# HGRN2 layer of a two-layer backbone: sum-free products first in the seven-product blocks, heads in a written order, four states in one PSUM bank

## The chip, the cores and the metric

The kernel runs on one core of one Trainium2 chip. The metric is the device time of one execution in microseconds (us). Before the change it is 3423.19 us, the median of 3 runs (3419.49 to 3425.61).

A core has five engines that run their own queues side by side. TensorE (PE) multiplies, VectorE (DVE) and GpSimd (POOL) work element by element, ScalarE (ACT) casts and evaluates functions, and SyncE (SP) issues most DMAs. An instruction waits at the head of its queue for semaphores of others, and what stands behind it in that queue waits too.

## The reference

Two layers over 1024 latent and 256 context tokens of width 1024. Layer 0 (neighbourhood attention beside an mLSTM) is not touched. Layer 1 is a bidirectional HGRN2 with 16 heads, key and value width 128 each:

```python
def _c_mixer(h_lat, h_ctx, w_in, lb, h_norm, w_out, need_ctx):
    def project(h):
        q, f_fwd, f_bwd, i, z = _split_cols(h @ w_in, C_SIZES)

        def decay(f_pre):
            f = lb + (1.0 - lb) * jax.nn.sigmoid(f_pre.astype(F32))
            return _bht(_heads(1.0 - f, HG_HEADS)), _bht(_heads(jnp.log(f), HG_HEADS))
        ...
    rec_l, z_l = project(h_lat)
    rec_c, z_c = project(h_ctx)
    o_l, o_c = _gla_bidir(rec_l, rec_c, need_ctx)
    ...

    def step(S, xs):
        qc, kc, vc, lfc = xs
        b = jnp.cumsum(lfc, axis=2)
        o = jnp.einsum('bhtk,bhkv->bhtv', qc * jnp.exp(b), S)
        pair = jnp.exp(jnp.where(tri, b[:, :, :, None, :] - b[:, :, None, :, :], -jnp.inf))
        a = jnp.einsum('bhtk,bhtsk->bhts', qc, pair * kc[:, :, None, :, :])
        o = o + jnp.einsum('bhts,bhsv->bhtv', a, vc)
        bL = b[:, :, -1:, :]
        S = jnp.exp(bL[:, :, 0])[..., None] * S + jnp.einsum('bhsk,bhsv->bhkv', kc * jnp.exp(bL - b), vc)
        return S, o
```

The gates f (forward and backward), q, values i and output gates z are projections of the normed tokens. In each direction a state S of 128 by 128 is carried from chunk to chunk; the context tokens give its start.

## The kernel before

**Products.** A dense fp32 product is three products of a high and a low part: hi by hi, hi by lo, lo by hi (`dense`, L131 to L133). `split` makes the parts: ScalarE casts (L73), VectorE subtracts (L74). So every weight block costs a cast and a subtraction before TensorE can use its low part.

**The passage into layer 1.** The normed tokens `hh`, `hl` (L317, L318) are made while layer 0's output projection ends. The backward gates of head 0 (`hg_f`, tiles mm, L983) are projected. Then `hg_wide` computes q and the forward gates of all heads in 16 blocks of two heads, each by seven products of half size instead of eight (one Strassen-like level). For this `half_sums` forms four sums S1 to S4 of quarters of the tokens (44 operations on VectorE, 12 on GpSimd, with the splits st1 to st4), and each block forms sums t1 to t4 of its weight quarters on GpSimd (L1072). The raw weights (`br`, DMAs at L1065) and the half sums share one ring of ten buffers. A unit of q comes first, and its products stand in the order (0,0), t2, (1,0), t3, t1, t4, (1,1). Products on S2 follow the first one. Their tails (L1048) add partial results; the forward-gate blocks also compute context parts of 256 columns (tiles tr). Results go to DRAM (`qd`, `fd`).

**A head.** `hg_intra` forms K = 1 - F (L1226), gkn (L1233), Q = q F (L1235), and then the causal matrix of each 128-token chunk in a binary scheme: the diagonal and seven levels. Each is a run of 16 strip matmuls (L1256); after it VectorE updates Q and K (L1303), F's running product (L1307), and merges the strips into gD (L1309). `hg_vz` projects context values, then values and output gates in eight token tiles of 24 products; `hg_close` transposes K (L1268); `hg_ctx` computes the states that the context gives (L1215); `hg_scan` carries the states. In the scan a u = K'V (L1323 backward, L1339 forward) goes into a PSUM bank of its own, three banks in turn, and VectorE makes the next state gS from it (L1325, L1341). The output acc sums three matmuls a chunk (L1334 to L1336), four chunks in the one acc bank, and VectorE multiplies it with the gate into gA (L1354). Transposes (L1393) follow. `hg_proj` loads the next head's q and f and projects its backward gates.

**Order.** Instructions are put on the engines by a scheduler that works on the written program with priorities: what is marked `urgent` (the strips) goes first, projections fill what is left. A pool's buffers are waited for as a whole unless it says otherwise.

## Time and profile before

| | before |
|---|---|
| median of 3 runs | 3423.19 us |
| the profiled execution: its time | 3423.08 us |
| its span | 3421.3 us |
| mean granted TensorE clock | 0.995 |
| DMA | 379.82 MB, mean 111 GB/s |

The span runs from the first to the last instruction in the trace. A row of a timeline gives start, time and the group of instructions, with the idle time ahead of it and what ended that in brackets. A row of the waits gives the waiting engine and line, who ended the wait, the sum, the number of times and the longest. A row of groups gives line, engine, operation, tiles, shapes and count, then busy time and the mean of one in ns. A row of the windows gives for each engine the busy time and the number of instructions in a stretch. Matmul records are pipelined, so their starts, not their lengths, give the pace.

### The profile page before, as it was taken

To read this page: it belongs to the slowest core of one execution; us is meant where nothing else is said; L and a number is where in the kernel's file an instruction comes from. 1 tells how busy PE (TensorE), PEld (TensorE's weight loads), DVE (VectorE), ACT (ScalarE), POOL (GpSimd) and SP (SyncE) were. 2 spreads that over 40 slices of the span, in tenths; PEclk is the share of its full clock that TensorE was granted. 3 is DMA by queue.
4 is the path that set the end of the run, shared out by engine and by line. 5 is a ranking of instruction groups with operands and counts; after the bars stand their busy time and mean duration, and the time that the engine had idled before them with its cause. 6 is when DMAs were issued, how large, how long until landed. Compare 5 with 4: busy or idle time off the path is not lost. (4 is left out here: it accounts for less than half of the span.)

```text
span 3421.3 us, 64930 instructions
## 1 busy us (share of the span) xinstructions
PE 3324.6 (97%) x24814; PEld 2927.6 (86%) x24814; DVE 2186.1 (64%) x4965; ACT 1454.6 (43%) x3389; POOL 834.7 (24%) x1215
## 2 busy tenths in 40 slices
PE   7999999999999999999997999999999999999999
PEld 6699899988899888898885888888888889889887
DVE  5346666666645576686667555665676576667757
ACT  5335554445534444454453333333333333333343
POOL 2222222222221121221015333112332242233110
PEclk9999999999999999999998999999999999999999
DMA  7612322223234443444742322322222233333357
GB/s 246 233 50 82 86 83 72 82 71 91 82 93 128 127 136 107 124 142 140 244 123 74 105 101 98 106 67 83 88 94 91 81 98 84 85 86 92 83 173 207
DMA packets 338103, 379.82 MB, mean 111 GB/s; under 512 B 34600, under 2 KB 269800, under 8 KB 336768
## 3 DMA queue, kind: packets, MB, share of 16 engines
q1 hardware_dynamic: 286032, 236.73, 23.6%
q0 software_dynamic: 51760, 138.94, 12.8%
q8 instruction: 195, 3.19, 0.4%
q14 instruction: 116, 0.95, 0.1%
HBM read 272.31 MB, written 103.08 MB: 110 GB/s over the span
## 5 line engine op out<-in xcount | busy, mean ns | idle before, releaser
L131 PE MATMUL mm<-wh,hh 128*128 128x256 f32 (+1 forms) x1504 | 464.2, 309 | 1.9 <-DVE graw L1535 0.7
L132 PE MATMUL mm<-wl,hh 128*128 128x256 f32 (+1 forms) x1504 | 462.9, 308 | 0.0
L133 PE MATMUL mm<-wh,hl 128*128 128x256 f32 (+1 forms) x1504 | 459.9, 306 | 0.0
L131 PE MATMUL mm<-hh,wh 128*128 128x512 f32 (+1 forms) x1096 | 400.3, 365 | 12.8 <-ACT wh L73 12.2
L133 PE MATMUL mm<-hh,wl 128*128 128x512 f32 (+1 forms) x1096 | 396.1, 362 | 3.1 <-DVE wl L74 3.1
L132 PE MATMUL mm<-hl,wh 128*128 128x512 f32 (+1 forms) x1096 | 396.9, 362 | 1.6 <-DVE hl L318 1.6
L131 PEld LDWEIGHTS mm<-wh,hh 128*128 128x128 f32 x1504 | 283.6, 189 | 21.1 <-ACT ev L352 3.4
L132 PEld LDWEIGHTS mm<-wl,hh 128*128 128x128 f32 x1504 | 283.6, 189 | 12.6 <-issue 0.7
L133 PEld LDWEIGHTS mm<-wh,hl 128*128 128x128 f32 x1504 | 283.5, 188 | 12.0 <-issue 0.5
L131 PE MATMUL mm<-wzh,hh 128*128 128x256 f32 x960 | 275.0, 287 | 0.7 <-DVE gz L1189 0.4
L132 PE MATMUL mm<-wzl,hh 128*128 128x256 f32 x960 | 275.2, 287 | 0.0
L133 PE MATMUL mm<-wzh,hl 128*128 128x256 f32 x960 | 274.8, 286 | 0.0
L131 PEld LDWEIGHTS mm<-hh,wh 128*128 128x128 f32 x1096 | 207.5, 189 | 47.9 <-ACT wh L73 12.6
L133 PEld LDWEIGHTS mm<-hh,wl 128*128 128x128 f32 x1096 | 207.2, 189 | 33.8 <-DVE wl L74 3.8
L132 PEld LDWEIGHTS mm<-hl,wh 128*128 128x128 f32 x1096 | 207.5, 189 | 31.9 <-DVE hl L318 4.3
L1286 ACT COPY gksel<-gK 128x1024 f32<-128x1024 f32 x96 | 110.8, 1154 | 193.8 <-PE s L1256 112.9
L131 PEld LDWEIGHTS mm<-wzh,hh 128*128 128x128 f32 x960 | 183.4, 191 | 2.7 <-DVE gz L1189 0.9
L132 PEld LDWEIGHTS mm<-wzl,hh 128*128 128x128 f32 x960 | 183.6, 191 | 1.6
L133 PEld LDWEIGHTS mm<-wzh,hl 128*128 128x128 f32 x960 | 183.4, 191 | 0.9
L1303 DVE TENSOR_TENSOR gQ<-gQ,gF 128x1024 f32<-128x1024 f32 x112 | 142.0, 1268 | 46.5 <-PE s L1256 46.1
L74 DVE TENSOR_TENSOR wl<-wraw,wh 128x512 fp32r<-128x512 f32 x176 | 120.0, 689 | 77.9 <-ACT wh L73 75.4
L1303 DVE TENSOR_TENSOR gK<-gK,gF 128x1024 f32<-128x1024 f32 x112 | 143.0, 1276 | 5.3 <-DVE gF L1307 0.5
(557 smaller groups left out, 8607.9 us busy)
## 6 DMA issues: line engine op xcount, KB each, us to landing
wraw<-in_wab_dram SPq DMA_DIRECT2D x108, 256.0 KB
wraw<-yd SPq DMA_DIRECT2D x92, 256.0 KB
br<-in_wc_dram SPq DMA_DIRECT2D x64, 256.0 KB
md<-ev POOLq DMA_DIRECT2D x60, 256.0 KB, 2.7
wraw<-in_wc_dram SPq DMA_DIRECT2D x120, 128.0 KB
mloz<-md SPq DMA_DIRECT2D x40, 256.0 KB
s<-gyt POOLq DMA_DIRECT2D x36, 256.0 KB, 5.0
adar<-in_wada_dram SPq DMA_DIRECT2D x16, 512.0 KB
```

The source lines that it names most:

```text
L74: nc.vector.tensor_tensor(out=lo, in0=x, in1=hi.bitcast(F32), op=ALU.subtract)
L131: mm(ps, lhsT=lh(k), rhs=rh(k), start=(start and k == 0), stop=False, skip_group_check=skip)
L132: mm(ps, lhsT=lh(k), rhs=rl(k), start=False, stop=False, skip_group_check=skip)
L133: m = mm(ps, lhsT=ll(k), rhs=rh(k), start=False, stop=(stop and k == nk - 1), skip_group_check=skip)
L1286: m = nc.scalar.copy(ksel.rearrange("p (b s i) -> p b s i", s=2, i=h), pick(K))
L1303: nc.vector.tensor_tensor(out=v, in0=v, in1=tot, op=ALU.mult)
```

## The change

**Half sums.** `half_sums` keeps its sums in the first half of F and in two working tiles instead of the ring, so the ring (now eleven) holds weights only; GpSimd's sum goes into output buffers. The counts of operations stay. It is called after the first three weight blocks have been asked for.

**Seven-product blocks.** A unit of gates comes first. Its products stand as (0,0), (1,0), t4, t2, t3, t1, then (0,1) and (1,1); t4 has an accumulator of its own. So three products and their context parts need no half sum. Tails are added in place. The pools wait tile by tile.

**Heads.** Context values (`hg_vt`) come ahead of the strips; each of the eight value tiles is issued after a strip run; the next head's gates are issued after the last run; the context states are placed after level 2; K's update stands ahead of a level's strips. In the scan four u's share one PSUM bank.

```diff
-    def half_sums(self, pool, tp):
+    def half_sums(self, pool, tp, F):
...
+        x = [F[:, 0, 0:512], F[:, 0, 512:1024]] + [self.t(tp, [P, 512], F32, n, 1) for n in ("u2", "u3")]
...
-        self.brs = 10
-        S = self.half_sums(sp, tp)
+        self.brs = 11
...
-        units = [(kind, i) for i in range(8) for kind in "qf"]
-        order = lambda kind: [(0, 0), "t2", (1, 0), "t3", "t1", "t4"] + ([(0, 1)] if kind == "f" else []) + [(1, 1)]
+        units = [(kind, i) for i in range(8) for kind in "fq"]
+        order = lambda kind: [(0, 0), (1, 0), "t4", "t2", "t3", "t1"] + ([(0, 1)] if kind == "f" else []) + [(1, 1)]
...
         more(3)
+        S = self.half_sums(sp, tp, F)
...
-            prod(pb, form("t2"), 2, True)
-            add(u2, pb, p1)
             w = form((1, 0))
             prod(pa, w, (0, 1), False)
             finish(0, 0, pa)
             cpart(0, w, 4, True)
+            prod(pd, form("t4"), (1, 1), True)
+            prod(pb, form("t2"), 2, True)
+            add(u2, pb, p1)
             prod(pb, form("t3"), 3, False)
             add(u3, pb, p1)
+            tail(1, 0, pd, u3, p1)
             prod(pc, form("t1"), 1, True)
-            tail(1, 1, pc, u3)
-            prod(pb, form("t4"), (1, 1), False)
-            tail(1, 0, pb, p1)
+            tail(1, 1, pc, u3, u3)
...
+    def hg_vz(self, st, pool, runs):
...
+        for tt in (6, 4, 2, 0):
 
             ps = self.ps("mm", [P, 2, 256])
             for j in range(2):
-                self.proj_nat(ps[:, j, :], w, tt + j, 0, 256)
+                with self.tc.issue_after(next(runs).ins):
+                    self.proj_nat(ps[:, j, :], w, tt + j, 0, 256)
...
+        runs = [m]
         for lev in range(7):
-            self.hg_level(hv, lev, pool)
-        return hv
+            runs.append(self.hg_level(hv, lev, pool))
+            if lev == 2:
+                S = self.hg_ctx(st, pool)
+        return hv, S, runs
...
                 if lev == 5:
                     self.level = m
+                update(K, 1, n - 1)
...
-            u = self.ps("s", [P, P])
+            if c in (7, 3):
+                u4 = self.ps("s", [P, 4, P])
+            u = u4[:, c % 4, :]
...
             if c % 4 == 0:
                 o4 = self.ps("acc", [P, 4, P])
+                u4 = self.ps("s", [P, 4, P])
...
             if c < 7:
-                u = self.ps("s", [P, P])
+                u = u4[:, c % 4, :]
...
-                with tc.tile_pool(name="st", bufs=1) as sp, tc.tile_pool(name="sx", bufs=1) as tp, self.pp.phase(x=4):
-                    self.hg_wide(sp, tp)
+                with tc.tile_pool(name="st", bufs=1, reuse_waits="tile") as sp, tc.tile_pool(name="sx", bufs=1, reuse_waits="tile") as tp, self.pp.phase(x=4):
+                    self.hg_wide(sp, tp, FF[0])
...
                 for h in range(16):
-                    hv = self.hg_intra(h, st, pool)
-                    self.hg_vz(h, st, pool, None if h else wv)
+                    self.hg_vt(h, st, pool, None if h else wv)
+                    hv, S, runs = self.hg_intra(h, st, pool)
+                    self.hg_vz(st, pool, runs)
                     self.hg_close(hv, pool)
-                    S = self.hg_ctx(st, pool)
                     self.hg_scan(st, hv, S, pool)
                     if h < 15:
-                        st = self.hg_proj(h + 1, pool)
+                        st = self.hg_proj(h + 1, pool, run=runs[7])
```

TensorE at the passage, as a piece of the difference: `mm_21655` is the last third of head 0's backward gates, on the newest tokens; `mm_21808` is the first product (0,0) of the first unit and `tr_21829` its context part.

```order
 L131 MATMUL mm_21655<-hh_20307,wh_20683 128x512
+L131 MATMUL mm_21808<-hh_20307,wh_21707 128x512
 L132 MATMUL mm_21655<-hl_20308,wh_20683 128x512
 L133 MATMUL mm_21655<-hh_20307,wl_20682 128x512
+L132 MATMUL mm_21808<-hl_20308,wh_21707 128x512
+L133 MATMUL mm_21808<-hh_20307,wl_21708 128x512
```

Products of the first unit now stand between the last gate products; before, all 24 gate products stood first, and the first products of the block behind them. Behind these rows follow in the new order the rest of `tr_21829`, then t4's and (1,0)'s products, and only then one on st2; the second unit's first two products stand ahead of the first unit's t3.

TensorE in the scan of one head, with the waits: `s` are the banks of the u's, `gkn` the transposed keys, `acc` the output bank, `gS` the states. Before (the rows follow the first u):

```order
L1323 MATMUL s_31393<-gv_31091,gkn_31348 128x128 [waits DVE_49]
L1323 MATMUL s_31397<-gv_31091,gkn_31348 128x128 [waits DVE_49]
L1323 MATMUL s_31401<-gv_31091,gkn_31348 128x128 [waits DVE_49]
L1323 MATMUL s_31405<-gv_31091,gkn_31362 128x128 [waits DVE_49]
L1323 MATMUL s_31409<-gv_31091,gkn_31362 128x128 [waits DVE_49]
L1323 MATMUL s_31413<-gv_31091,gkn_31362 128x128 [waits DVE_49]
L1339 MATMUL s_31421<-gv_31091,gkn_31355 128x128 [waits DVE_49]
L1339 MATMUL s_31428<-gv_31091,gkn_31355 128x128 [waits DVE_49]
L1335 MATMUL acc_31417<-gS_6101_31415,gQ_24864 128x128 [waits DVE_49]
```

And in the changed kernel (the rows end the run of backward u's of chunks 7 to 1, of which the first three are separated by some 20 projection products each):

```order
L132 MATMUL mm_31523<-hl_20308,wzh_31501 128x256
L133 MATMUL mm_31523<-hh_20307,wzl_31500 128x256
L1337 MATMUL s_31267<-gv_30774,gkn_31251 128x128 [waits DVE_49]
L1354 MATMUL s_31326<-gv_30774,gkn_31244 128x128 [waits DVE_49]
L1337 MATMUL s_31280<-gv_30774,gkn_31265 128x128 [waits DVE_49] x2
L1350 MATMUL acc_31290<-gS_5974_31288,gQ_24854 128x128 [waits DVE_49]
L1351 MATMUL acc_31290<-gS_5936_30923,gQ_24854 128x128
```

The u's of a half now name one bank (`s_31267`, `s_31280`) and stand apart, with projections between the first ones and nothing between the last.

TensorE ahead of the first strips of head 0: `mm_25145` is head 0's value projection, one of the tiles projected there before. Before:

```order
L132 MATMUL mm_25145<-wl_24826,hh_20307 128x256
L133 MATMUL mm_25145<-wh_24827,hl_20308 128x256
L131 MATMUL mm_25145<-wh_24827,hh_20307 128x256
L1256 MATMUL s_24876<-gq_24860,gkn_24865 64x64 [waits DMAHW5_49,DVE_49]
L1256 MATMUL s_24876<-gq_24860,gkn_24865 64x64 x7
```

And in the changed kernel, where `mm_24821` are the last six products of the context values; ahead of them stands the last product of the blocks, on st4:

```order
L133 MATMUL mm_24821<-hh_20307,wl_24798 128x256 [waits DVE_49]
L131 MATMUL mm_24821<-hh_20307,wh_24799 128x256
L132 MATMUL mm_24821<-hl_20308,wh_24799 128x256
L133 MATMUL mm_24821<-hh_20307,wl_24798 128x256
L1172 MATMUL tr_24848<-ident_82,gEc_24846 128x128 [waits Activation_49]
L1172 MATMUL tr_24848<-ident_82,gEc_24846 128x128
L1261 MATMUL s_24866<-gq_24818,gkn_24855 64x64 [waits DMAHW5_49,DVE_49,PE_49]
L1261 MATMUL s_24866<-gq_24818,gkn_24855 64x64 x7
```

Before, 82 projection products of 256 stood between the last product of the blocks and these strips; now six and two transposes do.

More of the change, by code (lines that the diff above doesn't have):

```diff
@@ L967, in gate_bc, with hg_f @@
             self.nc.sync.dma_start(out=self.gbc[:, v, :], in_=src.partition_broadcast(P))
-    def hg_f(self, h, pool, w=None):
+    def hg_f(self, h, pool, w=None, run=None):
         nc, a = self.nc, self.a
@@ L979, in hg_f @@
             ps = self.ps("mm", [P, n])
-            self.proj_tr(ps, w, 0, t0, n)
+            with self.tc.issue_after(run.ins) if run else ExitStack():
+                self.proj_tr(ps, w, 0, t0, n)
             dst = Fc[:, 1, :] if t0 == LAT else F[:, 1, t0 : t0 + 512]
@@ L984, in hg_f, with hg_proj @@
         return F, Fc
-    def hg_proj(self, h, pool, FF=None):
+    def hg_proj(self, h, pool, FF=None, run=None):
         dma = self.nc.sync.dma_start
-        F, Fc = FF or self.hg_f(h, pool)
+        F, Fc = FF or self.hg_f(h, pool, run=run)
         dma(out=F[:, 0, :], in_=self.fd[h, :, 0:LAT])
@@ L995, in hg_proj @@
         return dict(F=F, Fc=Fc, q=q)
-    def half_sums(self, pool, tp):
+    def half_sums(self, pool, tp, F):
         nc = self.nc
         hh, hl = self.hh, self.hl
-        S = {n: [self.t(pool, [P, 4, 512], F32R, f"st{n}{c}", 1) for c in "hl"] for n in range(1, 5)}
+        S = {n: [self.t(pool, [P, 4, 512], F32R, f"st{n}{c}", 1) for c in "hl"] for n in (4, 3, 1, 2)}
+        x = [F[:, 0, 0:512], F[:, 0, 512:1024]] + [self.t(tp, [P, 512], F32, n, 1) for n in ("u2", "u3")]
         def A(t, c, j):
@@ L1004, in A @@
             s = slice(512 * t, 512 * t + 512)
-            return hh[:, 4 * c + j, s].bitcast(F32), hl[:, 4 * c + j, s].bitcast(F32)
-        def done(n, j, x):
-            self.split(S[n][0][:, j, :], S[n][1][:, j, :], x)
-        def pair(eng, out, x, y, op):
-            e = self.t(tp, [P, 512], F32, "br", self.brs)
-            eng.tensor_tensor(out=out, in0=x[0], in1=y[0], op=op)
-            eng.tensor_tensor(out=e, in0=x[1], in1=y[1], op=op)
-            eng.tensor_tensor(out=out, in0=out, in1=e, op=ALU.add)
@@ L1016, in half_sums @@
-        tt = nc.vector.tensor_tensor
-        s1 = []
-        for j in range(4):
-            s1.append(self.t(tp, [P, 512], F32, "br", self.brs))
-            pair(nc.vector, s1[j], A(1, 0, j), A(1, 1, j), ALU.add)
-            done(1, j, s1[j])
-        s3 = []
-        for j in range(2):
-            s3.append(self.t(tp, [P, 512], F32, "br", self.brs))
-            pair(nc.gpsimd, s3[j], A(0, 0, j), A(1, 0, j), ALU.subtract)
+            return [y[:, 4 * c + j, s].bitcast(F32) for y in (hh, hl)]
@@ new lines, in chain, with done @@
+        def chain(eng, out, x0, x1, *rest):
+            eng.tensor_tensor(out=out, in0=x0, in1=x1[0], op=x1[1])
+            for y, op in rest:
+                eng.tensor_tensor(out=out, in0=out, in1=y, op=op)
+        def done(n, j, y):
+            self.split(S[n][0][:, j, :], S[n][1][:, j, :], y)
+        add, sub = ALU.add, ALU.subtract
+        for j in range(4):
+            (h, l), (h2, l2) = A(1, 0, j), A(1, 1, j)
+            chain(nc.vector, x[j], h, (l, add), (h2, add), (l2, add))
+            done(1, j, x[j])
@@ L1026, in half_sums @@
         for j in range(4):
-            for x in A(0, 0, j):
-                tt(out=s1[j], in0=s1[j], in1=x, op=ALU.subtract)
-            done(2, j, s1[j])
+            h, l = A(0, 0, j)
+            chain(nc.vector, x[j], x[j], (h, sub), (l, sub))
+            done(2, j, x[j])
         for j in range(4):
-            if j > 1:
-                s3.append(self.t(tp, [P, 512], F32, "br", self.brs))
-                pair(nc.gpsimd, s3[j], A(0, 0, j), A(1, 0, j), ALU.subtract)
-            done(3, j, s3[j])
+            (h, l), (h2, l2) = A(0, 0, j), A(1, 0, j)
@@ L1035, in half_sums, with hg_wide @@
+            y = self.t(tp, [P, 512], F32, "co", 2)
+            chain(nc.gpsimd, y, h, (l, add), (h2, sub), (l2, sub))
+            done(3, j, y)
         for j in range(4):
             h, l = A(0, 1, j)
-            tt(out=s1[j], in0=h, in1=s1[j], op=ALU.subtract)
-            tt(out=s1[j], in0=s1[j], in1=l, op=ALU.add)
-            done(4, j, s1[j])
+            chain(nc.vector, x[j], h, (x[j], sub), (l, add))
+            done(4, j, x[j])
         return S
-    def hg_wide(self, sp, tp):
+    def hg_wide(self, sp, tp, F):
@@ L1062, in raws @@
             b = {}
-            for r, c in ((0, 0), (0, 1), (1, 1), (1, 0)):
+            for r, c in ((0, 0), (1, 0), (0, 1), (1, 1)):
                 b[(r, c)] = self.t(tp, [P, 512], F32, "br", self.brs)
@@ L1076, in raws @@
             b["t2"] = sub(b[(1, 1)], b["t1"])
+            b["t4"] = sub(b[(1, 0)], b["t2"])
             b["t3"] = sub(b[(1, 1)], b[(0, 1)], None if kind == "f" else b[(0, 1)])
-            b["t4"] = sub(b[(1, 0)], b["t2"])
             return b
-        units = [(kind, i) for i in range(8) for kind in "qf"]
-        order = lambda kind: [(0, 0), "t2", (1, 0), "t3", "t1", "t4"] + ([(0, 1)] if kind == "f" else []) + [(1, 1)]
+        units = [(kind, i) for i in range(8) for kind in "fq"]
+        order = lambda kind: [(0, 0), (1, 0), "t4", "t2", "t3", "t1"] + ([(0, 1)] if kind == "f" else []) + [(1, 1)]
         queue = [(u, n) for u in range(len(units)) for n in order(units[u][0])]
@@ L1113, in finish, with tail @@
                 nc.gpsimd.dma_start(out=d[h, :, 512 * t : 512 * t + 512], in_=o)
-            def tail(t, c, ps, x):
-                o = self.t(tp, [P, 512], F32, "ct", 2)
-                add(o, ps, x)
-                finish(t, c, o)
+            def tail(t, c, ps, x, out):
+                add(out, ps, x)
+                finish(t, c, out)
             ctx = {}
@@ L1138, in cpart @@
                     nc.gpsimd.dma_start(out=self.fd[h, :, LAT:T], in_=o)
-            p1, u2, u3 = [self.t(tp, [P, 512], F32, n, 1) for n in ("p1", "u2", "u3")]
-            pa, pb, pc = self.ps("mm", [P, 512]), self.ps("x", [P, 512]), self.ps("x", [P, 512])
+            p1, u2, u3 = [self.t(tp, [P, 512], F32, n, 2 if n == "p1" else 1) for n in ("p1", "u2", "u3")]
+            pa, pd = [self.ps("mm", [P, 512]) for _ in range(2)]
+            pb, pc = [self.ps("x", [P, 512]) for _ in range(2)]
             w = form((0, 0))
@@ L1161, in hg_wide, with hg_vt @@
             prod(pc, w, 4, False)
-            tail(0, 1, pc, u2)
+            tail(0, 1, pc, u2, u2)
             cpart(1, w, 4, True)
-    def hg_vz(self, h, st, pool, w=None):
+    def hg_vt(self, h, st, pool, w=None):
         nc, a = self.nc, self.a
@@ L1169, in hg_vz @@
         w = w or self.wblock(pool, "wz", [col(3), col(4)], KD, 256)
-        st["ss"] = [self.t(pool, [P, 4], F32, "gss", 2) for _ in range(2)]
         v = self.t(pool, [P, NT, P], F32, "gv", 2)
-        z = self.t(pool, [P, NT - 2, P], F32, "gz", 1)
         ps = self.ps("mm", [P, CTX])
@@ L1180, in hg_vz @@
         nc.scalar.copy(v[:, 8:10, :], pt)
-        for tt in range(0, 8, 2):
+        st["v"], st["wz"] = v, w
+    def hg_vz(self, st, pool, runs):
+        nc, v, w = self.nc, st["v"], st["wz"]
+        st["ss"] = [self.t(pool, [P, 4], F32, "gss", 2) for _ in range(2)]
+        z = self.t(pool, [P, NT - 2, P], F32, "gz", 1)
+        runs = iter(runs)
+        for tt in (6, 4, 2, 0):
             ps = self.ps("mm", [P, 2, 256])
             for j in range(2):
-                self.proj_nat(ps[:, j, :], w, tt + j, 0, 256)
+                with self.tc.issue_after(next(runs).ins):
+                    self.proj_nat(ps[:, j, :], w, tt + j, 0, 256)
             nc.scalar.copy(v[:, tt : tt + 2, :], ps[:, :, 0:P])
@@ L1189, in hg_vz @@
             nc.vector.tensor_tensor(out=z[:, tt : tt + 2, :], in0=sg, in1=ps[:, :, P:256], op=ALU.mult)
-        st["v"], st["z"] = v, z
+        st["z"] = z
     def hg_ctx(self, st, pool):
@@ L1244, in hg_intra @@
                     o = c % 4 * P + b * 64
-                    self.strip(pa[:, c, :], b, ks[c // 4][:, o : o + 64], q[c // 4][:, o : o + 64])
+                    m = self.strip(pa[:, c, :], b, ks[c // 4][:, o : o + 64], q[c // 4][:, o : o + 64])
         nc.vector.tensor_tensor(
@@ L1248, in hg_intra @@
         )
+        runs = [m]
         for lev in range(7):
-            self.hg_level(hv, lev, pool)
-        return hv
+            runs.append(self.hg_level(hv, lev, pool))
+            if lev == 2:
+                S = self.hg_ctx(st, pool)
+        return hv, S, runs
     def strip(self, out, b, lhsT, rhs):
         s = slice(b * 64, (b + 1) * 64)
-        self.nc.tensor.matmul(out[s], lhsT=lhsT, rhs=rhs, start=True, stop=True, tile_position=(0, b * 64))
+        return self.nc.tensor.matmul(out[s], lhsT=lhsT, rhs=rhs, start=True, stop=True, tile_position=(0, b * 64))
     def hg_close(self, H, pool):
@@ L1282, in hg_level, with update @@
         out = self.ps("s", [P, 8, 64])
+        def update(t, o, step):
+            v = bass.AP(t.tensor, t.offset, [list(t.ap[0]), [n + h, 2], [2 * h, nb], [1, h]])
+            tot = bass.AP(Tt.tensor, Tt.offset + o, [list(Tt.ap[0]), [step, 2], [2, nb], [0, h]])
+            nc.vector.tensor_tensor(out=v, in0=v, in1=tot, op=ALU.mult)
         with self.urgent():
@@ L1298, in hg_level @@
                         rhs = Q[:, 1 - b, c * P + (1 - b) * 64 : c * P + (2 - b) * 64]
-                    self.strip(r, b, lhsT, rhs)
-            for t, o, step in ((Q, n + 1, -n - 1), (K, 1, n - 1)):
-                v = bass.AP(t.tensor, t.offset, [list(t.ap[0]), [n + h, 2], [2 * h, nb], [1, h]])
-                tot = bass.AP(Tt.tensor, Tt.offset + o, [list(Tt.ap[0]), [step, 2], [2, nb], [0, h]])
-                nc.vector.tensor_tensor(out=v, in0=v, in1=tot, op=ALU.mult)
+                    run = self.strip(r, b, lhsT, rhs)
+            update(Q, n + 1, -n - 1)
+            if lev == 6:
+                update(K, 1, n - 1)
             Tv = Tt[:, :, 0 : 2 * nb].rearrange("p d (b s) -> p d b s", s=2)
@@ L1309, in hg_level @@
             nc.vector.copy_predicated(D, self.lmask[:, lev + 1, :].unsqueeze(1).to_broadcast([P, 8, 64]), out)
-            return
+            return run
         for b in range(2):
@@ L1314, in hg_level @@
             nc.scalar.copy(A[s, :, e], out[s])
+        return run
     def hg_scan(self, st, H, S, pool):
@@ L1691, in build @@
                     )
-                pool = l1.enter_context(tc.tile_pool(name="hg", bufs=2))
+                pool = l1.enter_context(tc.tile_pool(name="hg", bufs=2, reuse_waits="tile"))
                 self.rawp = pool
```

## The prediction

> **What bounds the kernel now.** I read the busy table of the page first, then the busy time of stages cut by hand out of the span, then what TensorE waited for in the stages that have idle time, and the timeline there.

> ```profile
> PE 3324.6 (97%) x24814; PEld 2927.6 (86%) x24814; DVE 2186.1 (64%) x4965; ACT 1454.6 (43%) x3389; POOL 834.7 (24%) x1215
> core 0: us, PE busy (x) PEld busy (x) DVE busy (x) ACT busy (x) POOL busy (x), PEclk, DMA share, GB/s
> 1799.00:1848.50 49.50, 24.91 (x71) 16.54 (x72) 44.20 (x58) 18.85 (x42) 33.95 (x22) 0.69 0.16 48
> 1848.50:2195.60 347.10, 347.10 (x1692) 291.64 (x1691) 195.75 (x275) 122.63 (x211) 123.96 (x135) 1.00 0.30 101
> 2195.60:2263.80 68.20, 66.45 (x667) 61.04 (x666) 44.38 (x71) 24.39 (x42) 3.43 (x7) 1.00 0.30 93
> 2263.80:3222.50 958.70, 923.26 (x9352) 849.84 (x9352) 646.75 (x1029) 343.33 (x743) 278.72 (x383) 1.00 0.30 86
> ```

> TensorE bounds the kernel (97%). The change touches only layer 1, and there it can win in two places: the passage into the layer (1799 to 1848.5, half of it idle, mean granted clock 0.69) and the heads (2195.6 on). The seven-product stage between them has TensorE busy all through, so moving its products about gains nothing there.

> In the passage TensorE waits for weights and their splits:

> ```profile
> PE mm L131 <- ACT wh L73: 12.2, 1, 12.2
> PE x L131 <- ACT wh L73: 5.4, 2, 3.9
> PE mm L133 <- DVE wl L74: 3.1, 1, 3.1
> 1824.85 0.80 PE L131 MATMUL mm<-hh,wh 128*128 128x512 f32 x1 [12.19 <-ACT wh L73]
> ...
> 1842.19 0.63 PE L133 MATMUL x<-st2h,wl 128*128 128x512 f32 x1
> 1842.62 0.63 PE L131 MATMUL x<-st2h,wh 128*128 128x512 f32 x1
> ...
> 1846.52 0.40 PE L132 MATMUL mm<-hl,wh 128*128 128x512 f32 x1
> 1846.75 0.40 PE L133 MATMUL mm<-hh,wl 128*128 128x512 f32 x1
> SPq L1065 <- POOL br L1014: 18.6, 1, 18.6
> L1072 POOL TENSOR_TENSOR br<-br,br x1: 7067/7067/7067, 1828.0 to 1828.0; 128x512 f32<-128x512 f32 x1
> 1818.49 1.74 DVE L1028 TENSOR_TENSOR br<-br,hh 128x512 f32<-128x512 f32 x1
> ...
> 1821.82 0.68 DVE L1028 TENSOR_TENSOR br<-br,hh 128x512 f32<-128x512 f32 x1
> ...
> 1846.77 1.78 DVE L74 TENSOR_TENSOR st4l<-br,st4h 128x512 fp32r<-128x512 f32 x1
> ```

> Starts of neighbouring rows give the pace: a 512-wide product takes 0.23 us at full clock and 0.43 us at half. The weights come late because the DMA queue waits until sums give their buffers back. The sums come late because VectorE and GpSimd slow each other: the same addition takes 0.68 us alone and 1.74 us beside GpSimd, and a GpSimd subtraction stretches to 7.07 us. VectorE ends its last split at 1848.55. In these 49.5 us TensorE ran 71 records, 8 transposes of 0.11 us and 63 products: 15.4 us of work, so 34 us were lost.

> One head, at its scan (the rows of TensorE, then of VectorE):

> ```profile
> 2801.76 0.28 PE L133 MATMUL mm<-wzh,hl 128*128 128x256 f32 x1
> 2801.88 1.76 PE L1323 MATMUL s<-gv,gkn 128*128 128x128 f32 x10
> ...
> 2804.46 0.94 PE L1339 MATMUL s<-gv,gkn 128*128 128x128 f32 x4
> 2805.77 0.49 PE L1335 MATMUL acc<-gS,gQ 128*128 128x128 f32 x2 [0.37 <-DVE gS L1325]
> 2806.10 0.39 PE L1336 MATMUL acc<-gS,gQ 128*128 128x128 f32 x2
> 2806.32 0.39 PE L1334 MATMUL acc<-gv,gA 128*128 128x128 f32 x2
> ...
> 2809.86 1.15 PE L1256 MATMUL s<-gq,gkn 128*64 128x64 f32 x32 [0.25 <-DVE gS L1341]
> 2811.62 0.49 PE L1334 MATMUL acc<-gv,gA 128*128 128x128 f32 x2 [0.60 <-DVE gA L1354]
> ...
> 2815.47 0.88 PE L1256 MATMUL s<-gQ,gksel 128*64 128x64 f32 x16 [0.91 <-DVE gQ L1235]
> ...
> 2817.96 0.66 PE L1393 MATMUL tr<-ident,gA 128*128 128x128 f32 x4
> 2802.30 0.80 DVE L1325 SCALAR_TENSOR_TENSOR gS<-gS,gT,s 128x128 f32<-128x128 f32 x2 [0.90 <-PE s L1323]
> 2803.61 1.25 DVE L1325 SCALAR_TENSOR_TENSOR gS<-gS,gT,s 128x128 f32<-128x128 f32 x3
> ```

> A 128-wide fp32 matmul has two records, 0.22 us together (2806.10 to 2806.32); a run of 32 strip records takes 1.15 us; a 256-wide product takes 0.12 us (2801.76 to 2801.88). From 2801.88 to 2817.96 there are 72 such records (8.0 us) and 64 strip records (2.3 us): 10.3 us of work in 16.1 us, so **5.8 us are lost in each scan**, and with some 0.2 us elsewhere 6.0 us a head. The levels before it run gapless beside projections.

> **The change part by part.** The sum is made against the profiled execution, 3423.08 us, which lies 0.1 us from the median of 3423.19 us.

> *The passage.* The 44 VectorE and 12 GpSimd operations of the half sums stay, so the sums end at about the same time. What changes is what stands beside them. The weights no longer share the sums' buffers, and their pool waits tile by tile, so their DMAs need not wait until 1814.71. The first unit begins with three products that need no sum: 36 matmuls of 512 and 24 context matmuls of 256. As the order stands, the next context part (24 of 256), the two first products of the second unit (24 of 512) and one product that needs only the second sum (12) also stand ahead of what needs the later sums. That is 72 x 0.23 + 48 x 0.12 = 22.3 us of work, where before did 39 x 0.23 = 9.0 us by 1848.5. From there TensorE is saturated in both, so work done early is time saved: 13.3 us. Four more weight splits of 0.68 us fall on VectorE in that time, mostly covered by the extra work. I take **-13.0 us**. Bounds: at most the three waits above go, 20.7 us; at least 5 us, if four splits beside GpSimd take 1.74 us each and TensorE stands through that 7.0 us.

> The clock bears on it: after the 12.19 us wait the products run at 0.43 us. [...]

> *Inside the seven-product stage.* Same products, same sums in place, TensorE full. A product now waits for a tail of the unit before, but other products stand between. Nothing, -3 to +5: the stage has 195.75 us of VectorE in 347.10 as cover; without it a stalled VectorE addition costs its 0.68 us in each of 16 units, 11 us.

> *Head 0.* Before, 82 products of 256 stand ahead of its first strips; now the strips stand right behind the last seven-product matmul, with 6 products and 2 transposes (1.2 us) beside the chain.

> ```profile
> L1226 DVE TENSOR_SCALAR gK<-gF 128x2048 f32<-128x2048 f32 x14 | 17.2, 1227 | 36.8 <-PE tr L1268 36.8
> L1201 DVE TENSOR_TENSOR_SCAN gEc<-gFc,gzero 128x255 f32<-128x255 f32 x14 | 9.6, 683 | 0.0
> L1233 DVE TENSOR_TENSOR gkn<-gK 128x512 f32<-128x512 f32 x29 | 20.6, 710 | 0.2
> L1235 DVE TENSOR_TENSOR gQ<-gq,gF 128x512 f32<-128x512 f32 x60 | 49.3, 839 | 14.1 <-PE acc L1335 11.4 <-PE acc L1336 1.2
> L1303 DVE TENSOR_TENSOR gQ<-gQ,gF 128x1024 f32<-128x1024 f32 x98 | 125.0, 1275 | 38.9 <-PE s L1256 38.5
> ```

> VectorE then does an addition, a split and a gate sum (3 x 0.68), K = 1 - F (1.23), a scan (0.68) and two gkn (1.42): 5.4 us with no other work on TensorE than 1.2 us: 4.2 us lost. Behind it stand a second scan, four gQ (3.36) and an update of 1.28, then three operations of about 0.6 us before the context transposes, 7 us against 4.4 us of strips and projections; with handoffs I take 2.1 us. The loads of q wait for the same last product, but land under that chain. **+6.3 us**, between 0 (the projections that stood here fill another hole) and +10 (the q load of 256 KB is late).

> *Heads 1 to 15.* The same products change places: one value tile (24 products of 256, 2.9 us) behind each strip run and the next gates inside the scan. A level then has 2.9 + 1.15 = 4.0 us of TensorE. VectorE must have Q's update (1.28) done before the next strips, which fits under 2.9; the K update now stands ahead of the strips, also under them. If that cover is short by 0.2 us a level, it is 7 x 0.2 x 15 = 21 us. The scan: four states share a PSUM bank, and in the order each u waits for VectorE's read of the one before in its bank. A round trip, u to state to u, is 0.9 us (0.42 to VectorE's start, 0.35 of its own, the return), 0.68 more than the matmul. The projections cover the first three; the last four (fourth state, its bank's neighbours, first acc) have nothing between: 2.7 us. At the change of the acc bank u, gA and acc follow one another, 2.2 us; the second half of the level-0 strips 0.5; the context states, now between levels, 0.7. Together 6.1 us against 6.0: **+0.1 us a head, +1.5 us** for fifteen. Bounds: -1.5 (two of the four trips hidden) and +1.5 us (levels short), -22 to +22 us.

> *Last head and output projection.* The same operations, nothing put behind the strips: 0, give or take 3.

> **Sum:** 3423.1 - 13.0 + 6.3 + 1.5 = 3417.9 us, so **3418.0 us**. About 0.2% (6.8 us: under 3416.3, over 3430.0) is what a measurement of this kernel can tell from no change.

> **Rivals.**

> *The heads win.* If TensorE's queue takes the projections while VectorE works on the last four states, or the gates in the scan shorten the acc change too, each head gains 1.3 us: 15 x 1.4 = 21 less than the sum, 3397 us. For it: 5.8 us a scan are there to be had. Against it: the four waits stand next to each other in the order.

> *Slower: one bank for four states.* A u cannot start until the state before is read, where before three banks let u's run ahead (2801.88: 10 records in 2.1 us). If the round trip is paid seven times rather than four, or VectorE's gkn (0.71, between states at 2803.01) stands in it twice, each head loses 0.7 x 3 = 2.1, less 0.7 that the projections cover: 1.4 us a head, 21 us in all, 3437 us. It decides from 0.9 us a head. [...] The trace shows such a wait only at the acc bank (0.60 at 2811.62).

> *The passage does not open.* VectorE and GpSimd set its end and new weight splits lengthen them: a gain of 5 us, 3426 us.

> *The passage opens fully.* All 20.7 us go: 3410 us.

> **Chances.** Forecast 0.44 (its own range 3411 to 3425, 0.14 of it under 3416.3); heads win 0.20; one bank slower 0.17; passage closed 0.10 (0.03 of it over 3430); passage open 0.09. Faster 0.14 + 0.20 + 0.09 = 0.43; slower 0.17 + 0.03 = 0.20; same 0.37. The range 3400 to 3434 leaves out half of the heads' win and half of the slower case.

> **What the profile would show.** Right: the first weights' DMAs before 1800, no TensorE wait over 4 us in the passage, and the seven-product stage's end about 13 us earlier; four TensorE waits for gS at L1337 and L1350 of 0.4 us and more in each head; 4 us of idle ahead of the first strips; heads 67 to 68 us apart. Wrong: a head period under 66.3 us (the heads win) or over 68.9 us (bank or levels), TensorE waits for gQ at L1261 in the levels, or a wait of more than 5 us still in the passage.

## The result and the profile after

| kernel | median, us | before beside it, us | ratio, 95% interval |
|---|---|---|---|
| the changed kernel | 3440.56 (3439.37 to 3442.95, 4 runs) | 3422.36 | 1.0054 (1.0036 to 1.0071) |

The change makes the kernel 18 us slower. Its profiled execution has a span of 3437.3 us, 16.0 us over the one before. The page's row of the engines in the changed kernel:

```profile
PE 3329.7 (97%) x24814; PEld 2940.7 (86%) x24814; DVE 2179.7 (63%) x4965; ACT 1451.0 (42%) x3389; POOL 838.5 (24%) x1215
```

Its windows for the same stages as in the prediction (the passage, the rest of the blocks, head 0, heads 1 to 14; heads 1 and 15 begin here at their first strips):

```profile
core 0: us, PE busy (x) PEld busy (x) DVE busy (x) ACT busy (x) POOL busy (x), PEclk, DMA share, GB/s
1799.00:1848.50 49.50, 38.20 (x161) 30.54 (x162) 47.41 (x59) 20.21 (x43) 31.11 (x21) 0.83 0.09 28
1848.50:2182.20 333.70, 333.07 (x1619) 279.96 (x1617) 175.29 (x270) 117.94 (x204) 113.98 (x131) 1.00 0.31 101
2182.20:2249.50 67.30, 62.60 (x618) 57.60 (x618) 48.25 (x73) 23.89 (x40) 10.01 (x13) 0.95 0.33 101
2249.50:3219.80 970.30, 915.81 (x9213) 844.24 (x9212) 642.33 (x1014) 338.69 (x732) 277.90 (x372) 0.99 0.29 85
```

The passage holds 161 records of TensorE where it held 71, and the blocks end 12.5 us earlier (2182.1, before 2194.6). Then it is lost again: from the first strips of head 1 to those of head 15 the changed kernel takes 970.3 us, the one before 949.0 us (2268.2 to 3217.2) with 49 records more in it.

To compare stages with different records I give each record its pace (512-wide product 0.227 us, 256-wide 0.120, a 128-wide record 0.112, a transpose 0.109, a strip 0.044) and call the rest of a stage its lost time. A strip's pace here includes the switch to and from the strips (by the starts in both traces a run of 32 records takes 1.08 us, 0.034 a record, and one of 8 takes 0.44 us, 0.055 a record), so a little of the loss common to both kernels drops out; differences are sound.

| lost time, us | before | changed | difference | forecast |
|---|---|---|---|---|
| passage and blocks (from 1770) | 39.9 | 27.6 | -12.3 | -13.0 |
| head 0 | 4.0 | 8.3 | +4.3 | +6.3 |
| heads 1 to 14 | 51.6 | 78.8 | +27.2 | +1.4 |
| last head, output projection | 12.4 | 12.4 | 0.0 | +0.1 |

The sum is +19.2 us; the changed execution was 3.2 us of work ahead at 1770 already, at the end of layer 0, and so the span grows by 16.0 us. What TensorE waited for in the changed kernel's passage:

```profile
PE x L132 <- DVE st2l L74: 6.5, 2, 5.3
PE tr L294 <- DVE nx L282: 3.1, 1, 3.1
PE x L133 <- DVE wl L74: 1.3, 1, 1.3
```

And in its timeline the row of the DMA queue that loads the block weights:

```profile
1778.06 49.65 SPq L1059 DMA_DIRECT2D br<-in_wc_dram  x9
```

The weights start at 1778 instead of 1814.71, and of the waits for them only 1.3 us is left, for a low part (wl). The longest that remains is for the half sums (st2). From 1799 to 1848.5 TensorE does 30.5 us of work by the paces above, where it did 15.2; and from 1799 on, 17.1 us of the passage run at half clock, where 30.7 us did. In the heads, the waits of TensorE in heads 1 to 14 of the changed kernel are:

```profile
PE s L1354 <- DVE gS L1356: 19.1, 14, 1.4
PE s L1337 <- DVE gS L1339: 11.5, 29, 0.4
PE acc L1350 <- DVE gS L1339: 6.2, 14, 0.4
PE s L1354 <- DVE gS L1339: 6.2, 14, 0.4
PE s L1217 <- ACT gknc L1212: 5.0, 14, 0.4
PE acc L1349 <- DVE gA L1369: 4.8, 14, 0.7
```

And its timeline in one scan, without the projection rows:

```profile
2522.64 0.38 PE L1337 MATMUL s<-gv,gkn 128*128 128x128 f32 x2
2523.46 0.49 PE L1354 MATMUL s<-gv,gkn 128*128 128x128 f32 x2 [0.44 <-DVE gS L1339]
2524.32 0.49 PE L1337 MATMUL s<-gv,gkn 128*128 128x128 f32 x2 [0.37 <-DVE gS L1339]
2525.25 0.49 PE L1337 MATMUL s<-gv,gkn 128*128 128x128 f32 x2 [0.44 <-DVE gS L1339]
2526.18 0.49 PE L1350 MATMUL acc<-gS,gQ 128*128 128x128 f32 x2 [0.44 <-DVE gS L1339]
...
2533.11 0.39 PE L1354 MATMUL s<-gv,gkn 128*128 128x128 f32 x2
2534.91 0.49 PE L1354 MATMUL s<-gv,gkn 128*128 128x128 f32 x2 [1.41 <-DVE gS L1356]
2535.72 0.49 PE L1349 MATMUL acc<-gv,gA 128*128 128x128 f32 x2 [0.33 <-DVE gA L1369]
```

Read the starts: a matmul of this form takes 0.22 us. From 2522.64 to 2526.18 four of them take 3.54 us, so 2.66 us are lost in four round trips to VectorE; from 2533.11 to 2535.72 two take 2.61 us, 2.17 us lost at the change of the acc bank. The waits come in every head (14 times each, 29 for the second row).

### The profile page after: what moved, and what is told of

The parts are those of the page before. It is cut to its first block, busy times and chain, and to the rows that moved or that the text cites. A ratio compares the mean times of both kernels' runs of the same rounds, so it can differ in the third digit from the quotient of the medians.

```text
span 3437.3 us, 64829 instructions
## 1 busy us (share of the span) xinstructions
PE 3329.7 (97%) x24814; PEld 2940.7 (86%) x24814; DVE 2179.7 (63%) x4965; ACT 1451.0 (42%) x3389; POOL 838.5 (24%) x1215
## 4 chain that ended last, share of the span: by engine, by line
PE 85%; DVE 4%; issue 4%; DMA 3%; ACT 2%; POOL 1%; SPq 1%; DVEq 0%; POOLq 0%; ACTq 0%
PE mm L131 16%; PE mm L132 15%; PE mm L133 15%; PE s L1261 4%; PE mm L923 3%; PE mm L924 3%; PE mm L925 3%; PE acc L861 2%; PE tr L841 2%; PE acc L633 2%; PE s L642 2%; PE x L133 1%; PE x L131 1%; PE x L132 1%; PE acc L1350 1%
## 5 line engine op out<-in xcount | busy, mean ns | idle before, releaser
L131 PE MATMUL mm<-wh,hh 128*128 128x256 f32 (+1 forms) x1504 | 466.2, 310 | 2.2 <-DVE graw L1550 0.8
L132 PE MATMUL mm<-wl,hh 128*128 128x256 f32 (+1 forms) x1504 | 464.1, 309 | 0.0
L133 PE MATMUL mm<-wh,hl 128*128 128x256 f32 (+1 forms) x1504 | 461.6, 307 | 0.0
L131 PE MATMUL mm<-hh,wh 128*128 128x512 f32 (+1 forms) x1160 | 421.7, 364 | 4.7 <-DVE og L959 3.1
L132 PE MATMUL mm<-hl,wh 128*128 128x512 f32 (+1 forms) x1160 | 422.9, 365 | 0.0
L133 PE MATMUL mm<-hh,wl 128*128 128x512 f32 (+1 forms) x1160 | 422.3, 364 | 0.4 <-DVE wl L74 0.4
L131 PEld LDWEIGHTS mm<-wh,hh 128*128 128x128 f32 x1504 | 284.8, 189 | 21.4 <-ACT ev L352 3.4
L132 PEld LDWEIGHTS mm<-wl,hh 128*128 128x128 f32 x1504 | 284.9, 189 | 12.3 <-issue 0.7
L133 PEld LDWEIGHTS mm<-wh,hl 128*128 128x128 f32 x1504 | 284.7, 189 | 12.0 <-issue 0.5
L131 PE MATMUL mm<-wzh,hh 128*128 128x256 f32 x960 | 284.8, 297 | 0.0
L133 PE MATMUL mm<-wzh,hl 128*128 128x256 f32 x960 | 272.6, 284 | 0.0
L132 PE MATMUL mm<-wzl,hh 128*128 128x256 f32 x960 | 272.4, 284 | 0.0
L131 PEld LDWEIGHTS mm<-hh,wh 128*128 128x128 f32 x1160 | 219.3, 189 | 41.7 <-ACT ev L371 4.2
L133 PEld LDWEIGHTS mm<-hh,wl 128*128 128x128 f32 x1160 | 219.2, 189 | 33.1 <-DVE wl L74 1.0
L132 PEld LDWEIGHTS mm<-hl,wh 128*128 128x128 f32 x1160 | 219.5, 189 | 29.7 <-issue 0.2
L131 PEld LDWEIGHTS mm<-wzh,hh 128*128 128x128 f32 x960 | 183.3, 191 | 7.2
L132 PEld LDWEIGHTS mm<-wzl,hh 128*128 128x128 f32 x960 | 184.2, 192 | 0.0
L133 PEld LDWEIGHTS mm<-wzh,hl 128*128 128x128 f32 x960 | 183.5, 191 | 0.0
L74 DVE TENSOR_TENSOR wl<-wraw,wh 128x512 fp32r<-128x512 f32 x176 | 120.1, 690 | 74.9 <-ACT wh L73 71.7
L1292 DVE TENSOR_TENSOR gK<-gK,gF 128x1024 f32<-128x1024 f32 x112 | 152.3, 1360 | 6.7
```

The lines of the kernel that those rows point to most:

```text
L74: nc.vector.tensor_tensor(out=lo, in0=x, in1=hi.bitcast(F32), op=ALU.subtract)
L131: mm(ps, lhsT=lh(k), rhs=rh(k), start=(start and k == 0), stop=False, skip_group_check=skip)
L132: mm(ps, lhsT=lh(k), rhs=rl(k), start=False, stop=False, skip_group_check=skip)
L133: m = mm(ps, lhsT=ll(k), rhs=rh(k), start=False, stop=(stop and k == nk - 1), skip_group_check=skip)
L1292: nc.vector.tensor_tensor(out=v, in0=v, in1=tot, op=ALU.mult)
```

## The experiments

Twelve kernels were run, each beside the kernel before. The theories after the result: **banks** (the four states in one bank cost the heads their time) and **order** (moving the projections uncovered the levels or the scan). Times are medians.

| run | what it is | us | before beside it | ratio, 95% interval |
|---|---|---|---|---|
| e1_front | passage and blocks changed, heads as before | 3415.67 | 3425.19 | 0.9971 (0.9960 to 0.9981) |
| e2_heads | heads changed, the rest as before | 3456.11 | 3425.19 | 1.0083 (1.0066 to 1.0100) |
| e3_banks | changed, one bank for each u | 3364.95 | 3425.19 | 0.9819 (0.9805 to 0.9834) |
| e4_u4_alone | before, four u's a bank | 3553.66 | 3425.19 | 1.0369 (1.0354 to 1.0385) |
| e5_back4 | e3, backward u's four a bank | 3428.59 | 3423.37 | 1.0009 (1.0000 to 1.0019) |
| e6_fwd4 | e3, forward u's four a bank | 3409.05 | 3423.37 | 0.9947 (0.9932 to 0.9962) |
| e7_pairs | e3, two u's a bank | 3392.11 | 3423.37 | 0.9900 (0.9886 to 0.9915) |
| e8_gates_free | e3, gates not bound behind the last strips | 3368.03 | 3423.37 | 0.9825 (0.9808 to 0.9842) |
| e9_ctx_back | e3, context states behind the closing again | 3405.06 | 3426.15 | 0.9944 (0.9929 to 0.9959) |
| e10_values_free | e3, value tiles not bound behind strip runs | 3495.52 | 3426.15 | 1.0211 (1.0195 to 1.0226) |
| e11_head0_free | e3, head 0's value tiles not bound | 3367.11 | 3426.15 | 0.9835 (0.9818 to 0.9851) |
| e12_k_behind | e3, K's update behind the strips | 3362.61 | 3426.15 | 0.9822 (0.9807 to 0.9837) |

**The two halves of the change.** e1 takes the heads' functions and their loop from the kernel before:

```diff
-                    self.hg_vt(h, st, pool, None if h else wv)
-                    hv, S, runs = self.hg_intra(h, st, pool)
-                    self.hg_vz(st, pool, runs)
+                    hv = self.hg_intra(h, st, pool)
+                    self.hg_vz(h, st, pool, None if h else wv)
                     self.hg_close(hv, pool)
+                    S = self.hg_ctx(st, pool)
```

> The passage and the seven-product blocks as changed, the heads (strips, values, scan, their order) as before. If the passage's gain stands by itself, the time is 3422.4 - 12.3 (the passage's lost time is 39.9 us before and 27.6 us in the changed kernel) = 3410 us, 3405 to 3414. If the gain is eaten later, because the heads then meet their loads or head 0 loses its cover anyway, 3418 to 3424 us.

e2 is the other half: `hg_f`, `hg_proj`, `hg_vt`, `hg_vz`, `hg_intra`, `hg_level`, `hg_scan` and the loop of the changed kernel, in the kernel before.

> The passage and the blocks as before, the heads as changed. If the parts add up, the heads cost 27 us in heads 1 to 14 and 4 us in head 0: 3422.4 + 31 = 3453 us, 3447 to 3459. If the heads only lose because the earlier passage puts them in another position, 3430 us or less.

e1 came out 9.5 us under the kernel before beside it, just over its range of 3405 to 3414; its trace has lost 26.8 us in passage and blocks, 13 less than before. e2 came out 30.9 us over it, as expected. The halves add up (-9.5 and +30.9 against +18.2 for both), so the passage's gain is real and the heads lose by themselves.

**Banks or order.** e3 takes back only the shared bank:

```diff
-            if c in (7, 3):
-                u4 = self.ps("s", [P, 4, P])
-            u = u4[:, c % 4, :]
+            u = self.ps("s", [P, P])
...
-                u4 = self.ps("s", [P, 4, P])
...
-                u = u4[:, c % 4, :]
+                u = self.ps("s", [P, P])
```

> The changed kernel with one PSUM bank for each u again (three in turn); all else as changed. Theory of the banks: the last four states go from 0.9 us a step to 0.42 us, 1.9 us a head less, and the halved clock in the heads goes too: 3440.6 - 28 = 3412 us, 3408 to 3420. Theory of the order (the moved projections leave levels and scan uncovered, the banks are a side matter): 3436 to 3441 us.

It is 60 us faster than the kernel before and 76 us faster than the changed one, far outside either range. The waits of TensorE in its heads 1 to 14 (the whole list):

```profile
PE s L1261 <- DVE gQ L1237: 6.2, 11, 0.6
PE s L1261 <- DVE gS L1353: 4.3, 15, 1.0
PE s L1351 <- DVE gS L1353: 0.7, 2, 0.4
PE s L1261 <- DVE gQ L1292: 0.2, 1, 0.2
```

And one scan in its timeline, without the projection rows:

```profile
2488.65 0.83 PE L1335 MATMUL s<-gv,gkn 128*128 128x128 f32 x6
2493.66 0.83 PE L1335 MATMUL s<-gv,gkn 128*128 128x128 f32 x6
2498.35 0.38 PE L1335 MATMUL s<-gv,gkn 128*128 128x128 f32 x2
2498.57 0.61 PE L1351 MATMUL s<-gv,gkn 128*128 128x128 f32 x4
```

The backward u's go in threes (six records), one a bank, and VectorE makes three states while TensorE runs the projections between (4 us and more). No row waits any more for a state in the scan but at its end. The heads lie 63.9 us apart; lost time in heads 1 to 14 is 2.9 us in all. So the **banks** lose the time, and the new **order** by itself takes out nearly all that the kernel before loses in its heads (51.6 us). With its banks the change gives that back and 27 us more.

e4 is the same edit the other way round, in the kernel before (`hg_scan` alone from the changed kernel).

> The kernel before with four u's a bank and nothing else changed. Theory of the banks: the six backward u's behind the first now go at 0.9 us instead of 0.42 us: 2.9 us a head, 16 heads, 3422.4 + 46 = 3468 us, 3450 to 3470. Theory of the order: 3422 to 3430 us, because projections fill the steps or the chain was not what ended last.

It is 128 us slower, beyond the range of the banks' theory. The window of its heads 1 to 14:

```profile
2267.40:3333.70 1066.30, 980.38 (x9261) 893.22 (x9260) 626.38 (x1012) 342.00 (x734) 253.26 (x372) 0.94 0.27 77
```

Its mean clock is 0.94 there. Counted in the trace, 131 us of the stretch run at half clock, which is 64 us of the 117 us that these heads lose more than before, against the 3.4 us at half clock before. The other 53 us are 3.8 us a head, where 2.9 us was expected. The expectation counted the backward u's alone and left out the clock.

**The price of a shared bank.** Three kernels share banks in part:

```diff
-            if c in (7, 3):
-                u4 = self.ps("s", [P, 4, P])
-            u = u4[:, c % 4, :]
+            if c in (7, 5, 3, 1):
+                u2 = self.ps("s", [P, 2, P])
+            u = u2[:, c % 2, :]
```

This is the backward side of e7; the forward side is alike. e5 shares four a bank on the backward side alone, e6 on the forward side alone.

> The changed kernel with four backward u's a bank, forward u's in banks of their own. Base: 3365 us with all u's in banks of their own. Theory of round trips: each backward u that waits for the read of the one ahead in its bank costs its own 0.6 to 0.7 us, 2.7 us a head in the trace, 15 heads: 3365 + 40 = 3405 us, 3398 to 3412. Rival (one serial chain: any one of the two sides already brings the whole loss): 3430 to 3441 us.

> The changed kernel with four forward u's a bank, backward u's in banks of their own. Theory of round trips: the waits at the change of the acc bank, 1.6 + 0.6 us a head in the trace, 15 heads: 3365 + 33 = 3398 us, 3390 to 3405; with the backward side the two add to the whole. Rival (one serial chain): 3430 to 3441 us.

> The changed kernel with two u's a bank on both sides. Theory of round trips: half of the u's wait, some 2 us a head: 3365 + 30 = 3395 us, 3383 to 3405. Rival (what counts is how many banks are free ahead, and pairs leave more free than single ones): 3362 to 3372 us.

e7 (+27 us over e3) lies in the range of the round trips, and pairs are no free ring. But half of its u's do not wait: its backward u's wait 0.2 us in heads 1 to 14 together, and its rows are the first acc of the scan (5.2 us), the forward u's (3.2 us) and the strips behind the last forward state (13.6 us). So its time came out for a cause only partly the expected one. e5 (+64) and e6 (+44) lie above their ranges, and together above the changed kernel (+76). The clock is why. In e5 the windows of 3.4 us around 2387, 2455 and 2523, with what lies between:

```profile
2385.40:2388.80 3.40, 3.40 (x16) 3.40 (x17) 2.30 (x4) 0.00 (x0) 0.00 (x0) 0.50 0.00 0
2388.80:2453.60 64.80, 62.39 (x645) 57.84 (x644) 42.94 (x69) 24.34 (x52) 19.54 (x27) 1.00 0.30 93
2453.60:2457.10 3.50, 3.50 (x17) 3.50 (x18) 2.26 (x4) 0.00 (x0) 0.00 (x0) 0.51 0.02 5
2457.10:2521.90 64.80, 62.40 (x645) 57.85 (x644) 44.45 (x69) 24.35 (x52) 19.57 (x27) 1.00 0.30 93
2521.90:2525.30 3.40, 3.40 (x18) 3.40 (x18) 2.10 (x4) 0.00 (x0) 0.00 (x0) 0.50 0.00 0
```

The figure behind the five engines is the granted clock: half in each of the three short windows, which stand right behind the four waits. Each half window loses some 1.7 us, an estimate: half of its 3.4 us. Taken together over heads 1 to 14:

| | lost time over e3, us | at half clock, us | lost to the clock (half of it) | left, per head | waits in the trace, per head |
|---|---|---|---|---|---|
| e5, backward shared | 57.5 | 41.0 | 20.5 | 2.64 | 2.66 |
| e6, forward shared | 41.1 | 27.3 | 13.7 | 1.96 | 2.17 |
| changed kernel, both | 75.8 | 15.9 | 7.9 | 4.85 | 4.83 |

The clock's part is an estimate, half of the time at half clock. Without it the two sides nearly add up (4.60 against 4.85 us a head), and each costs about what its round trips are. A serial chain in which one side already brings the whole does not hold.

**What the order gains.** Four parts of it were taken back one at a time, in e3. The gates:

```diff
-                        st = self.hg_proj(h + 1, pool, run=runs[7])
+                        st = self.hg_proj(h + 1, pool)
```

> The changed kernel with a bank for each u, and the next head's gates not bound behind the last strip run. Theory of cover in the scan (the 72 gate products between the u's are what takes the 3.7 us a head out that the kernel before loses): 3365 + 50 = 3415 us, 3400 to 3420. Rival (the value tiles behind the strips bring it, the gates would come late anyway): 3362 to 3372 us.

The context states:

```diff
-            if lev == 2:
-                S = self.hg_ctx(st, pool)
-        return hv, S, runs
+        return hv, runs
...
                     self.hg_close(hv, pool)
+                    S = self.hg_ctx(st, pool)
```

> The changed kernel with a bank for each u (base 3365 us), the context states back behind the closing of the head. If their place between the levels is part of what the new order gains (48 us against the old order of the heads, 3.3 us a head): 3378 us or more. If their place is a side matter: 3361 to 3371 us.

The value tiles:

```diff
-                with self.tc.issue_after(next(runs).ins):
-                    self.proj_nat(ps[:, j, :], w, tt + j, 0, 256)
+                self.proj_nat(ps[:, j, :], w, tt + j, 0, 256)
```

> The changed kernel with a bank for each u (base 3365 us), the eight value tiles not bound behind strip runs. Theory of the value tiles (they are the cover between strip runs, and what they leave goes into the scan): the old loss comes back, 3365 + 45 = 3410 us, 3395 to 3420. Rival (the priorities put them there anyway): 3362 to 3371 us.

K's update:

```diff
-                update(K, 1, n - 1)
...
             update(Q, n + 1, -n - 1)
-            if lev == 6:
-                update(K, 1, n - 1)
+            update(K, 1, n - 1)
```

> The changed kernel with a bank for each u (base 3365 us), K's update behind the strips of its level again. Theory of a short cover (1.28 us more in the chain from strips to strips than 2.9 us of value products hide with Q's 1.28 us and handoffs): 0.2 us a level, 3365 + 21 = 3386 us, 3376 to 3400. Rival (the cover holds): 3362 to 3370 us.

Freeing the gates (+3 us) and moving K's update (-2 us) change nothing that a run can tell. For the gates this is the rival's case: in e8's trace the gate products stand between the backward u's without the binding too (in the head at 2511, 19 and 10 of them behind the first two groups of u's; in e3's head at 2505, 19 and 16). What they are worth as cover was therefore not tested. The place of the context states is worth 40 us, the binding of the value tiles 130 us, far more than the 45 us that was expected of them. One scan of e9 in its timeline, without the projection rows, and then the waits of TensorE in e10's heads (the whole list):

```profile
2507.41 1.06 PE L1217 MATMUL s<-gv,gknc 128*128 128x128 f32 x8
2508.31 0.39 PE L1333 MATMUL s<-gv,gkn 128*128 128x128 f32 x2
2510.57 1.76 PE L1333 MATMUL s<-gv,gkn 128*128 128x128 f32 x10
2512.70 0.49 PE L1333 MATMUL s<-gv,gkn 128*128 128x128 f32 x2 [0.37 <-DVE gS L1335]
2513.15 0.94 PE L1349 MATMUL s<-gv,gkn 128*128 128x128 f32 x4
2515.01 0.49 PE L1345 MATMUL acc<-gS,gQ 128*128 128x128 f32 x2 [0.92 <-DVE gS L1335]
```

```profile
PE s L1260 <- DVE gQ L1291: 103.1, 27, 7.3
PE s L1260 <- ACT gksel L1296: 2.2, 1, 2.2
```

In e9 the context states (L1217) stand at the end of the projections that the scan could have hidden behind. The chain of states starts when they are there, and runs in one piece with nothing beside it, as in the kernel before. In e10 the value products are used up early, so that the late strip runs stand bare and wait for Q's update, up to 7.3 us each, and 157 us of these heads run at half clock, which costs some 78 us.

**Head 0.** The binding of the value tiles was lifted there:

```diff
-                with self.tc.issue_after(next(runs).ins):
+                run = next(runs)
+                with self.tc.issue_after(run.ins) if h else ExitStack():
                     self.proj_nat(ps[:, j, :], w, tt + j, 0, 256)
```

> The changed kernel with a bank for each u (base 3365 us), value tiles bound from head 1 on only, in head 0 free. Theory of head 0 (4 us idle ahead of its first strips and 7 us at half clock behind, 3.5 us): 3365 - 6 = 3359 us, 3355 to 3362. Rival (free tiles do not move ahead of the strips there): 3363 to 3368 us.

No gain, though not for the reason that the rival gave. What TensorE waited for in the strips of head 0, in e3 (its two largest rows) and then in e11:

```profile
PE s L1261 <- DMA gq<-qd: 2.7, 1, 2.7
PE s L1261 <- ACT gksel L1297: 0.9, 1, 0.9
```

```profile
PE s L1262 <- DVE gQ L1293: 4.4, 2, 3.0
PE s L1262 <- ACT gksel L1298: 2.6, 1, 2.6
```

The tiles did move ahead of the strips and took their wait away, but then the later levels had none left, and the wait came back there (7.0 us), with 13.7 us at half clock from 2217 on, where e3 has 6.8 us at the start of head 0.

e3 and e12 beat both kernels: 3364.95 and 3362.61 us, which cannot be told apart.

## Why the prediction was wrong

**The passage: right.** -13.0 us forecast, -12.3 in the trace, and -9.5 us alone in e1 (an interval of -14 to -6 us). The weights come early and the sum-free products fill the hole, as the step said. A wait of 5.3 us is left (for st2), which the text named as a sign of failure; the gain stood all the same, since other products had gone ahead.

**The blocks, the last head: right,** nothing to speak of. **Head 0: right in kind, near in size partly by luck,** +4.3 against +6.3. TensorE waits 3.5 us ahead of the first strips (2.1 of it for gkn) where 4.2 was worked out, and from these strips to the scan no wait is left where 2.1 was taken. In its place 6.8 us run at half clock, 3.4 us lost, which the sum did not have.

**The changed heads' two main waits: right to a tenth.** Four trips 2.7 us, 2.66 measured; the acc change 2.2, 2.17 measured; they add up (4.85 us a head in the table above). The context states cost 0.4 us a head (L1217) where 0.7 was taken. The levels held: no wait for gQ between them in the changed kernel.

**What failed is the line "6.1 us against 6.0: +0.1 us a head".** Measured it is +1.9 us a head (27.2 over 14). Two terms of it were off:

- *The 6.0 us of before.* They were taken from one scan, at 2801.88, with 5.8 us lost. By the same working (its paces, from the first u to the first L1393) the scans of heads 1 to 14 lose between 2.0 and 6.4 us, 4.6 in the mean: the term was 1.2 us a head too large. The waits over heads 1 to 14 would have told it; their main rows in the kernel before:

```profile
PE acc L1334 <- DVE gA L1354: 8.6, 14, 0.7
PE s L1256 <- DVE gQ L1235: 7.7, 10, 0.9
PE acc L1335 <- DVE gS L1325: 6.3, 14, 0.7
PE s L1323 <- DVE gS L1325: 5.2, 14, 0.4
PE s L1256 <- DVE gS L1341: 3.5, 13, 0.6
```

  That is 31.3 us in 14 heads, 2.2 us a head, where the five kinds of wait together made 3.3 us in that one scan: the wait for gQ comes 10 times in 14 heads, and there it came twice. The fourth row also corrects a reading: a u, which reads no state, waits for its bank once a head in the kernel before too, though the prediction saw such a wait only at the acc bank.
- *The clock.* The step counted waits alone. Five half windows fell into the changed heads where one fell before: 15.9 against 3.4 us, 6.2 us lost, 0.45 a head.

Together 1.2 + 0.45 = 1.65 of the 1.84 us a head by which the line was off (27.2 over 14, less the 0.1). The remaining 0.2 us a head is not assigned.

**Behind the failed line stands a net of two large terms.** The step priced the heads as a whole and found nothing. The runs split it: the order takes out 48.7 us of lost time in heads 1 to 14 (51.6 before, 2.9 in e3), the shared bank puts in 75.8 us. The rival "one bank for four states" named the right cause, and nearly the time (3437; measured 3440.6) by luck, since its reason was wrong: seven trips or gkn between them were not needed, four and the acc change were enough against a before that loses less. The rival "the heads win" was the other half of the truth: without the bank it is 3365 us, 32 us under what it gave. The forecast was a net of two such terms, and an error of a third in the larger one is enough to turn its sign.

**The text's own tests** told it apart: a head period over 68.9 us (69.3 measured) with no waits for gQ in the levels points to the bank.

## What to carry to other kernels

Where a change both reorders work and shares a buffer, price the two apart: a good order can hide what a shared buffer then brings back. A bank that held several states of a chain made each matmul wait here until the vector engine had read the state ahead (0.6 to 0.7 us each), unless enough other work stood between (2.3 us of projections ahead of the u at 2522.64, and no wait); count those waits in the written order. Take the loss of a repeated stage from all of its repetitions, not from the one that is shown.

## What the runs showed of the hardware

In one scan of the changed kernel TensorE went to half clock with no wait over 0.44 us ahead of it. These two windows follow each other there:

```profile
2313.00:2316.50 3.50, 1.80 (x10) 1.04 (x8) 2.05 (x6) 1.15 (x2) 0.00 (x0) 1.00 0.00 0
2316.50:2319.90 3.40, 3.40 (x18) 3.17 (x20) 1.94 (x3) 0.00 (x0) 0.00 (x0) 0.50 0.00 0
```

I counted, by the paces above, the work in each stretch between two such multiples, for the 735 stretches at full clock from 2150 us on in these two traces. The 4 with less than 0.35 of a full stretch's work were each followed by a half window, 3 of the 10 with 0.35 to 0.44 were, and none of the other 721. In the changed kernel the stretch at the four waits holds 0.23 at 2313.08 and 0.36 at 2453.03, with a half window behind each, and 0.43 at 2384.76 and 0.39 at 2729.51, with none. These are counts of two traces; no run was made to find a limit.
